# Two hybrid decoder layers on Trainium2: mixer steps cut to 128 columns and traced in another order

## The chip, the cores and the metric

The kernel runs on one core of a Trainium2 chip. The metric is the device time of one execution in microseconds. Engines: PE (TensorE, matmuls), DVE (VectorE), ACT (ScalarE), POOL (GpSimd), and SP, whose queue issues the DMA transfers.

## What is computed

Two layers of a decoder trunk act on x of 256 tokens by 1024 features, modulated by a conditioning vector c. In short:

```python
for l in range(2):
    sh_m, sc_m, g_m, sh_f, sc_f, g_f = split(silu(c) @ ada_w[l] + ada_b[l])
    h = rms_norm(x, norm_mix[l]) * (1 + sc_m) + sh_m
    rw_cols, ssd_cols, fox_cols, gate_logits = split(h @ w_in[l])
    y_rw  = rwkv7(rw_cols)    # token shift, decay, delta-rule state over 256 steps, 8 heads of 64
    y_ssd = ssd(ssd_cols)     # conv of 4 taps, chunked state-space scan, 16 heads in 4 groups
    y_fox = fox(fox_cols)     # causal softmax attention with forget gates, 8 heads
    merged = sum(sigmoid(gate_b) * (y_b @ proj_b))
    x = x + g_m * (merged @ w_out[l])
    h = rms_norm(x, norm_ffn[l]) * (1 + sc_f) + sh_f
    x = x + g_f * FFN(h)      # layer 0: SwiGLU; layer 1: the best 2 of 8 SwiGLU experts
```

All products are in float32 precision: both operands are split into a high and a low part, and three matmuls of the parts are summed.

## The kernel before, in words

Time runs through six stages: start, mixer of layer 0 (about 60 to 485 us of the span), its output projection and the dense FFN, mixer of layer 1 (about 720 to 1165 us), its output projection, and the experts.

A **mixer** consists of steps that share the engines. Every weight block comes by a DMA from SP's queue into one of three `raw` tiles. `accumulate` (L369) has ACT copy it to the high part (L157) and DVE subtract to the low part (L158), each 128x512 at a time, into five pairs of tiles; then PE multiplies 24 times for 128 columns (8 blocks of 128 features, three products each, 256 tokens wide). `stationary` (L379) does that for two blocks of 128 columns and calls what evacuates each from PSUM. PSUM has two `pd` banks for projections, four `pm` and two `ps`.

The steps and their names in the order string:
- `rw` and `r0`, `r1`: `rwkv_half` (L489) does four heads. Stages: projections of k, r and v with token shift (L451, L452), then the decay and key work up to masked matrices (L515 to L620; the mask copies are L615 on DVE), then the **levels** (L627 to L699), state and output (L700 to L752), gating (L753 to the end). The levels invert a triangular matrix in six doublings. In each, POOL masks (L632), PE multiplies, DVE transposes 32x32 blocks out of PSUM (L658), PE multiplies, DVE adds (L665), PE transposes, ACT copies (L675). The next doubling needs the result.
- `sd` and `s0` to `s3`: `ssd_group` (L798) with three stages: four blocks of projection with convolution (L808, L811, L813, L814), the chunk products (L831 to L867), the gate columns (L873 to L875) and the norm.
- `fx` and `f0`, `f1`: `fox_half` (L913): q, k and v by `project_rows` (L393), then attention of two pairs of heads.
- `G`: `gates` (L980), the first branch's gate columns, evacuated at L978. `m0`, `m1`, `m2`: `merge` (L989), the three branches' gate and output columns, evacuated at L1008 or L1010 and L1011.
- `mo` and `md`: `mod_next` (L293) loads 512 columns of a later modulation weight (L211) and sums them on DVE (L224, L226). `gm` puts a modulation row together.

Each of these functions is a generator, and `stages` (L438) makes the next call go on to the next `yield`. The loop at L1389 walks through `ORDER[l]` (L51) and runs one stage for each word. The string thus sets the order in which instructions are traced. The program is built with `schedule_with_timeline_sim=True`: a list scheduler then fixes the order of instructions on each engine, in which an instruction traced earlier goes first among those that are ready. On the chip each engine follows its fixed order and waits on semaphores.

Of the kernel before, what the change touches and what calls it, by code (L numbers as in the profile page):

```python
# [18 lines left out]
P = 128  # L19
# [44 lines left out]
def trunk(  # L64
# [314 lines left out]
    def stationary(raw, n, evac):  # L379

        ps = dbank()
        for q in range(0, n, P):
            m = min(P, n - q)
            o = ps[:m, q * 2:q * 2 + T]
            accumulate(o, raw[:, :, q:q + m], (hh, hl))
            evac(q // P, o)

    def project_cols(wsrc, c0, n, evac):
        for p0 in range(0, n, 256):
            w = min(256, n - p0)  # L390
            stationary(load_raw(rows(wsrc, 0, D, c0 + p0, w), KD, w), w, lambda i, ps: evac(p0 // P + i, ps))

    def project_rows(wsrc, c0, y):  # L393
# [3 lines left out]
        for kg in range(4):  # L397
            hi, lo = split_part(raw[:, 2 * kg:2 * kg + 2, :])
            for t in range(2):
                tb = slice(t * P, (t + 1) * P)  # L400
                for k in range(2):
                    kt = 2 * kg + k
                    mm3(ps[t], (y[0][:, kt, tb], y[1][:, kt, tb]), (hi[:, k, :], lo[:, k, :]), kt == 0, kt == KD - 1)
        return ps
# [67 lines left out]
    def rwkv(mx, l, prm, lora, gl):  # L472
        wa = mx("wa", [P, T])
        project_cols(w_in[l], 1536, 256, lambda i, ps: shift(prm, wa if i == 0 else gl[:, 0, :], ps, 12 + i))
# [12 lines left out]
        return [y[:, 0], y[:, 1]], lambda jp: stages(rwkv_half)(mx, l, prm, lora, jp, wa, gl, vup, y)  # L487

    def rwkv_half(mx, l, prm, lora, jp, wa, gl, vup, y):  # L489
# [8 lines left out]
        for dst, g in ((k, 1), (r, 0), (v, 2)):  # L498
            project_cols(w_in[l], g * RW + jp * 256, 256, lambda i, ps: shift(prm, dst[:, i, :], ps, 4 * g + 2 * jp + i))
# [11 lines left out]
        yield  # L511

        s, th = u(), u()
        for jj in J:
            js = slice((2 * jp + jj) * P, (2 * jp + jj + 1) * P)  # L515
            for dst, hb, base in ((s, 0, W0), (th, 1, A0)):
                ps = mbank()[:, :T]
                mm(ps, wau[hblock(hb), js], wa[hblock(hb), :])
                act.activation(dst[:, jj, :], ps, AF.Tanh, scale=0.5, bias=col(pph, base, jj))
        dve.tensor_scalar_add(s, s, 1.0)  # L520
# [10 lines left out]
        dve.tensor_tensor(L8, L8, mid.unsqueeze(2).broadcast_to([P, 4, P]), op=ALU.subtract)  # L531
        e1, e3, e2 = u(), u(), u()
# [4 lines left out]


# [6 lines left out]
        for t in range(2):  # L545
            for jj in J:
                mm(ps[:, t * 4 + 2 * jj:t * 4 + 2 * jj + 2], sq[:, jj, t * P:(t + 1) * P], headsel)
        ss, rs = small(8, "r"), small(8, "r")
# [9 lines left out]


# [10 lines left out]
        for jj in J:  # L570
            cv = "p (c t) -> p c t"
            dve.scalar_tensor_tensor(ar[jj][:, :, 0, :], kk[:, jj, :].rearrange(cv, c=2), -1.0, e2[:, jj, :].rearrange(cv, c=2), op0=ALU.mult, op1=ALU.mult)
            dve.tensor_mul(ar[jj][:, :, 1, :], r[:, jj, :].rearrange(cv, c=2), e1[:, jj, :].rearrange(cv, c=2))
        rk = u()
# [8 lines left out]


# [11 lines left out]

        s0 = mx("s0", [P, 2, 64])
# [5 lines left out]
        for ch in range(2):  # L603
# [4 lines left out]
            for dst, src in ((mats[:, 0], bt), (mats[:, 1], kt)):  # L608
# [29 lines left out]
        for ch in range(2):  # L638
# [4 lines left out]
            tms.append(tm)  # L643
        for ch in range(2):
            pz = level(ch, 0, icomp)
            tts[ch] = sq128()
            dve.tensor_add(tts[ch], pz, icomp)
        for ch in range(2):
# [3 lines left out]
            act.activation(tls[ch], pz, AF.Copy)  # L652
        for lv in range(1, 6):
            odd = slice(1, 4, 2) if lv == 5 else slice(0, 4)
            for ch in range(2):
                pz = level(ch, lv, tls[ch])
                for q in range(4):
                    dve.transpose(blk(bds[ch], q)[:, odd, bcol(q)], by4(blk(pz, q))[:, odd, :])  # L658
            for ch in range(2):
# [7 lines left out]
                else:  # L667
                    for n in (1, 3):
                        act.activation(blk(tms[ch], n)[:, :, bcol(n - 1)], by4(blk(pz, n)), AF.Copy)
            for ch in range(2):  # L670
# [5 lines left out]
                if lv == 4:  # L676
                    for n in range(4):
                        pool.tensor_copy(blk(tms[ch], n)[:, :, bcol(n)], by4(blk(tls[ch], n)))
        for ch in range(2):
# [4 lines left out]
            act.activation(ums[ch], pz, AF.Copy)  # L684
        h0, h1 = slice(0, 64), slice(64, 128)
        yas = []
        for ch in range(2):
# [4 lines left out]
            act.activation(yas[ch][h1], py[h1], AF.Copy)  # L692
        for ch in range(2):
# [5 lines left out]
        yield  # L699
        for ch in range(2):  # L700
# [23 lines left out]
            act.activation(sa, psa[:, 0:4, :], AF.Copy)  # L724
            if ch == 0:
# [12 lines left out]


# [10 lines left out]
            dve.tensor_scalar(var, var, 1.0 / 64, GN_EPS, op0=ALU.mult, op1=ALU.add)  # L750
            rsq(rs, var)
            dve.tensor_tensor(yg, yg, bc(rs), op=ALU.mult)  # L752
        yield  # L753
        pg = mbank()
        for jj in J:
            js = slice((2 * jp + jj) * P, (2 * jp + jj + 1) * P)
            mm(pg[:, jj * T:(jj + 1) * T], gu0[:, js], gl[:, 0, :], True, False)
            mm(pg[:, jj * T:(jj + 1) * T], gu1[:, js], gl[:, 1, :], False, True)
        yt = u()
# [11 lines left out]
    def ssd(mx, l, prm, dtr):  # L771
# [24 lines left out]
        return [yh, yl], lambda g: stages(ssd_group)(mx, l, prm, g, dt, cum, ac, dte, yh, yl)  # L796

    def ssd_group(mx, l, prm, g, dt, cum, ac, dte, yh, yl):  # L798
# [20 lines left out]
        stationary(raw, 256, lambda i, ps: conv(2 + i, ps))  # L819
        project_cols(w_in[l], XBC_OFF + g * 256, 256, conv)  # L820

        yield
# [7 lines left out]
        for ch in range(2):  # L830
            dve.tensor_tensor(xdt[:, ch, :].rearrange(h64, f=64), ps[:, ch, :].rearrange(h64, f=64),  # L831
                              hc(dt, ch).unsqueeze(2).broadcast_to([P, 4, 64]), op=ALU.mult)

# [5 lines left out]
        act.activation(cb[:, 2, :], ps[:, 1, :], AF.Copy)  # L839

        wms = [sv(4, P) for _ in range(3)]
        for b in range(2):
# [5 lines left out]
            for e in range(2):  # L848
# [3 lines left out]
                act.activation(wms[2][:, h, :], pc[:, e, 1, :], AF.Exp, bias=dte[:, 4 * g + h:4 * g + h + 1])  # L852
        for i in range(3):
            if i < 2:
                act.activation(wms[i], wms[i], AF.Exp, scale=-1.0)
            dve.tensor_tensor(wms[i], wms[i], cb[:, i, :].unsqueeze(1).broadcast_to([P, 4, P]), op=ALU.mult)
        y1 = sv(2, T)
# [11 lines left out]
        yield  # L869
# [7 lines left out]
        project_cols(w_in[l], SSD_OFF + g * 256, 256, gate)  # L877
# [8 lines left out]
        dve.tensor_scalar(ss, ps[:, 0:2], 1.0 / 256, EPS, op0=ALU.mult, op1=ALU.add)  # L886
        rsq(rs, ss)
# [9 lines left out]
    def fox(mx, l, prm, dtr):  # L897
# [13 lines left out]
        return [y[:, 0], y[:, 1]], lambda hf: stages(fox_half)(mx, l, qg, sums, hf, y)  # L911

    def fox_half(mx, l, qg, sums, hf, y):  # L913
# [3 lines left out]
        for g in range(3):  # L917
            ps = project_rows(w_in[l], FOX_OFF + 16 + g * 512 + hf * 256, (hh, hl))
# [11 lines left out]
            qkv.append(o)  # L930
        dve.tensor_scalar(ss, ss, 1.0 / 64, EPS, op0=ALU.mult, op1=ALU.add)
# [4 lines left out]
        for jj in range(2):  # L936
            yield
            j = 2 * hf + jj
            ka, qa = unit(mx, 2, T), unit(mx, 2, T)
            for e in range(2):  # L940
# [6 lines left out]
                act.activation(qa[0:65, e, :], ps[0:65, T:], AF.Copy, scale=qg[0:65, 0:1])  # L947
            po = mbank()[:, :T]
            for t in range(2):
                n = P * (t + 1)  # L950
                psc = mbank().rearrange("p (e k) -> p e k", e=2)
                for e in range(2):
                    mm(psc[:, e, :n], qa[0:65, e, t * P:(t + 1) * P], ka[0:65, e, :n], True, False)
                    mm(psc[:, e, t * P:n], identb, nmq, False, True)
                nmx, sm, rc = small(2, "f", 9), small(2, "f", 9), small(2, "f", 9)
# [5 lines left out]
                dve.tensor_tensor(pr[:, :, :n], pr[:, :, :n], rc.unsqueeze(2).broadcast_to([P, 2, n]), op=ALU.mult)  # L961
                pt = mbank().rearrange("p (e s q) -> p e s q", e=2, s=2)
# [550 lines left out]
```

## Time and profile before

| | us |
|---|---|
| median of 3 runs (lowest, highest) | 2197.69 (2197.65, 2198.89) |
| the profiled execution's own time | 2193.99 |
| its span, first to last instruction | 2192.2 |
| PE, DVE, ACT, POOL busy | 2075.0, 1799.2, 1380.4, 155.5 |
| instructions | 35360 |

The busy times overlap, so they add up to more than the span. A matmul counts as busy from its start to the modelled end of its result, so PE can be counted busy although it could take more. PEclk is the clock that TensorE was granted, as a share of its full speed. Line numbers are those of the kernel before.

### The profile page before, as it was taken

Reading aid. Unit: us, or ns where it says so; the run is one execution under the profiler, and the core shown is the slowest. Engines: PE = TensorE matmul, PEld = TensorE weight load, DVE = VectorE, ACT = ScalarE, POOL = GpSimd, SP = SyncE. Lnnn points to the kernel's source line nnn. Section 1 sums busy time; section 2 is a strip of 40 time slices with the busy share of each in tenths; the row PEclk is TensorE's granted clock in tenths of the full one; section 3 lists DMA queues with packets and bytes.
Section 4 is the critical chain, followed back from the end, with each engine's and each line's share of the span. In section 5 each row is a group of like instructions: output and inputs, shape, how many; then the busy total and the mean of one; then the engine's idle time right before and its main releaser. Section 6 shows DMA issues by size and latency. Waiting matters only on the chain.

```text
span 2192.2 us, 35360 instructions
## 1 busy us (share of the span) xinstructions
PE 2075.0 (95%) x13301; PEld 1797.9 (82%) x13301; DVE 1799.2 (82%) x2822; ACT 1380.4 (63%) x2204; POOL 155.5 (7%) x187
## 2 busy tenths in 40 slices
PE   6888899999997979989998999999999999999998
PEld 4778799999996868869998788888888887888776
DVE  4877777778776797857768999999999989998887
ACT  3445465555454536536556787777788777777775
POOL 2211210000000031210002000000000000000000
PEclk8999999999998889999998999999999999999999
DMA  8433355667884333415567999999999999999994
GB/s 292 126 94 90 96 177 191 204 211 256 285 290 157 113 100 107 145 49 169 190 198 261 349 372 355 329 348 385 368 332 365 354 350 352 338 352 367 343 352 168
DMA packets 313874, 546.77 MB, mean 249 GB/s; under 512 B 9856, under 2 KB 141056, under 8 KB 313696
## 3 DMA queue, kind: packets, MB, share of 16 engines
q1 hardware_dynamic: 313696, 544.44, 71.8%
q8 instruction: 106, 1.74, 0.3%
q14 instruction: 72, 0.59, 0.1%
HBM read 543.36 MB, written 1.05 MB: 248 GB/s over the span
## 4 chain that ended last, share of the span: by engine, by line
PE 80%; DVE 12%; issue 3%; DMA 3%; ACT 2%; POOL 0%; SPq 0%; DVEq 0%; ACTq 0%; POOLq 0%
PE pd L123 38%; PE pm L123 32%; PE ps L123 7%; DVE lo L158 5%; DVE u L658 2%; PE pm L132 2%; DMA araw<-in_ada_w_dram 1%; PE ps L132 1%; ACT hi L157 1%; DVE cu L811 1%; DMA b<-in_ada_w_dram 1%; DMA raw<-in_moe_w_gu_dram 0%; DVE b L615 0%; DVE xr L1270 0%; DMA raw<-in_proj_ssd_dram 0%
## 5 line engine op out<-in xcount | busy, mean ns | idle before, releaser
L157 ACT ACTIVATE hi<-raw 128x1024 fp32r<-128x1024 f32 (+2 forms) x1200 | 1024.6, 871 | 496.0 <-PE pd L123 257.0
L158 DVE TENSOR_TENSOR lo<-raw,hi 128x1024 fp32r<-128x1024 f32 (+2 forms) x1196 | 1153.9, 992 | 194.4 <-ACT hi L157 176.2
L123 PE MATMUL pd<-hh,hi 128*128 128x256 f32 (+1 forms) x1184 | 350.2, 296 | 20.8 <-DVE cu L811 5.2
L123 PE MATMUL pd<-hl,hi 128*128 128x256 f32 (+1 forms) x1184 | 342.2, 289 | 0.8 <-DVE hl L365 0.8
L123 PE MATMUL pd<-hh,lo 128*128 128x256 f32 (+1 forms) x1184 | 341.2, 289 | 0.0
L123 PE MATMUL pm<-lo,hh 128*128 128x512 f32 x672 | 266.7, 397 | 2.7 <-DVE lo L158 2.5
L123 PE MATMUL pm<-hi,hh 128*128 128x512 f32 x672 | 265.9, 396 | 0.3 <-ACT hi L157 0.2
L123 PE MATMUL pm<-hi,hl 128*128 128x512 f32 x672 | 262.4, 391 | 0.0
L123 PEld LDWEIGHTS pd<-hh,hi 128*128 128x128 f32 (+1 forms) x1184 | 231.9, 196 | 34.8 <-issue 7.2
L123 PEld LDWEIGHTS pd<-hl,hi 128*128 128x128 f32 (+1 forms) x1184 | 232.7, 196 | 5.7 <-DVE hl L365 2.7
L123 PEld LDWEIGHTS pd<-hh,lo 128*128 128x128 f32 (+1 forms) x1184 | 232.2, 196 | 2.1 <-issue 1.3
L123 PE MATMUL pd<-lo,hi 128*128 128x512 f32 x448 | 175.0, 391 | 0.0
L123 PE MATMUL pd<-hi,hi 128*128 128x512 f32 x448 | 169.9, 391 | 0.0
L123 PE MATMUL pd<-hi,lo 128*128 128x512 f32 x448 | 168.2, 390 | 0.0
L123 PEld LDWEIGHTS pm<-lo,hh 128*128 128x128 f32 x672 | 126.3, 188 | 32.3 <-DVE lo L158 5.8
L123 PEld LDWEIGHTS pm<-hi,hh 128*128 128x128 f32 x672 | 126.2, 188 | 29.3 <-ACT hi L157 1.4
L123 PEld LDWEIGHTS pm<-hi,hl 128*128 128x128 f32 x672 | 126.3, 188 | 26.1
L123 PE MATMUL pm<-hi,more 128*128 128x512 f32 x448 | 142.0, 392 | 0.0
L123 PEld LDWEIGHTS pd<-hi,hi 128*128 128x128 f32 x448 | 84.1, 188 | 18.2 <-ACT hi L407 0.3
L123 PEld LDWEIGHTS pd<-hi,lo 128*128 128x128 f32 x448 | 84.0, 188 | 17.8 <-DVE lo L408 0.2
L123 PEld LDWEIGHTS pm<-hi,more 128*128 128x128 f32 x448 | 84.1, 188 | 17.5 <-ACT hi L157 0.3
L123 PEld LDWEIGHTS pd<-lo,hi 128*128 128x128 f32 x448 | 84.1, 188 | 17.5
(429 smaller groups left out, 3428.7 us busy)
## 6 DMA issues: line engine op xcount, KB each, us to landing
raw<-in_moe_w_gu_dram SPq DMA_DIRECT2D x224, 1024.0 KB, 6.9
raw<-in_moe_w_down_dram SPq DMA_DIRECT2D x110, 1024.0 KB, 6.9
raw<-in_w_in_dram SPq DMA_DIRECT2D x66, 1024.0 KB, 5.4
araw<-in_ada_w_dram SPq DMA_DIRECT2D x68, 512.0 KB, 4.7
raw<-in_ffn_w_gu_dram SPq DMA_DIRECT2D x22, 1024.0 KB, 7.3
raw<-in_ffn_w_down_dram SPq DMA_DIRECT2D x11, 1024.0 KB, 6.6
raw<-in_w_in_dram SPq DMA_DIRECT2D x16, 512.0 KB, 5.2
raw<-in_proj_ssd_dram SPq DMA_DIRECT2D x8, 1024.0 KB, 5.4
```

What stands on the lines that cost most here:

```text
L123: pe.matmul(o, lhsT, rhs, start=start, stop=stop)
L132: pe.transpose(o, i, ident[:n, :n])
L157: act.activation(hi, raw, AF.Copy)
L158: minus.tensor_sub(lo, raw, hi.bitcast(F32))
L658: dve.transpose(blk(bds[ch], q)[:, odd, bcol(q)], by4(blk(pz, q))[:, odd, :])
L811: dve.scalar_tensor_tensor(cu[:, s:T], ps[:, 0:T - s], pph[:, w:w + 1], cu[:, s:T], op0=ALU.mult, op1=ALU.add)
```

## The change

The mixers' functions yield more often: after each 128-column block of a projection, and between the parts of the RWKV, SSD, FoX and gate work. One RWKV half has 56 steps in place of 5, one SSD group 14 in place of 3, one run of gates or merges 8 in place of 4. `stages` is gone, and `small_cols` becomes a word of the string (`sc`). The instructions are the same. `ORDER` becomes two strings in which `r0*47` means 47 steps in a row.

```diff
-ORDER = [
-    (
-        "rw r0 r0 mo r0 r0 fx sd s0 s0 s0 s1 s1 s1 r1 r1 r1 r0 s2 mo s2 s2 f0 r1 r1 s3 mo G f0 mo G s3 s3 G "
-        "f0 G m0 f1 m0 f1 m0 md md m1 md m0 m1 m1 md f1 md md md m1 m2 gm m2 md m2 m2"
-    ).split(),
-    (
-        "rw r0 r0 mo r0 sd s0 s0 r0 r0 s0 s1 mo s1 s1 s2 r1 r1 G r1 s2 fx r1 G s2 r1 G s3 s3 mo f0 f0 s3 G m0 "
-        "f0 m0 mo m0 m0 f1 md f1 m1 m1 md md md gm m1 md m1 f1 m2 m2 m2 md md md m2"
-    ).split(),
-]
+ORDER = (
+    "sc rw r0*7 mo r0*47 fx sd s0*13 s1*5 r1*6 s1*3 r1*14 s1*5 s0 s1 r1*7 r0 r1*9 r0 s2*2 f0 s2*2 r1*5 s2*3 f0*3 r1 f0*2 r1*7 s2*3 mo s2*2 r1*2 s2 r1*2 s3*2 f0 s3 r1*2 mo G*2 f0*2 s3*2 f0*4 mo G*2 s3 r1 s3*5 s2 s3*3 G*2 f0*9 G f1 G f1 m0*3 f1 m0 f1*6 m0*2 f1 md f1*3 m1*3 md m1 md m0*2 m1*3 md f1*8 md m1*5 md m1*2 md f1 m1*2 m2*4 gm m2*4 md m2*8",
+    "sc rw r0*21 mo r0*8 sd r0*3 s0 r0 s0*3 r0 s0 r0 s0 r0*2 s0*3 r0 s0 r0*18 s0*4 s1*5 mo s1*7 s2 s1 s2*4 r1*6 s1 r1*13 G*2 r1*4 s2 fx r1*7 G s2 r1*2 s2*2 r1*17 s2*5 r1*2 G r1*4 s3 G*2 r1 s3*8 f0 mo f0*3 s3 f0*10 s3*4 G*2 m0*2 f0*8 m0*2 mo m0*2 f1 m0*2 f1*5 md f1*5 m1*4 f1*3 m1*4 md*3 gm m1*4 md m1*4 f1*8 m2*12 md*3 m2*4",
+)
...
             accumulate(o, raw[:, :, q:q + m], (hh, hl))
             evac(q // P, o)
+            yield
...
-    def stages(f):
-
-        def start(*a):
-            g = f(*a)
-            return lambda: next(g, None)
-        return start
+    def whole(g):
+
+        while True:
+            try:
+                next(g)
+            except StopIteration as e:
+                return e.value
...
         for dst, g in ((k, 1), (r, 0), (v, 2)):
-            project_cols(w_in[l], g * RW + jp * 256, 256, lambda i, ps: shift(prm, dst[:, i, :], ps, 4 * g + 2 * jp + i))
+            yield from project_cols(w_in[l], g * RW + jp * 256, 256, lambda i, ps, g=g, dst=dst: shift(prm, dst[:, i, :], ps, 4 * g + 2 * jp + i))
...
-            for step in ORDER[l]:
+            for word in ORDER[l].split():
+                name, _, n = word.partition("*")
+                for _ in range(int(n or 1)):
+                    take(name)
```

## Rows read from the trace of the kernel before

**Rows 1.** The page: busy time, share of the span and instructions of each engine.

```profile
PE 2075.0 (95%) x13301; PEld 1797.9 (82%) x13301; DVE 1799.2 (82%) x2822; ACT 1380.4 (63%) x2204; POOL 155.5 (7%) x187
```

**Rows 2.** Stretches: length; busy (count) PE, PEld, DVE, ACT, POOL; clock, DMA share, GB/s.

```profile
60.00:290.00 230.00, 204.08 (x1830) 178.59 (x1830) 181.01 (x403) 111.77 (x268) 52.59 (x59) 0.94 0.35 106
735.00:1000.00 265.00, 233.38 (x2027) 204.10 (x2026) 210.31 (x456) 131.96 (x312) 58.50 (x62) 0.92 0.36 106
...
60.00:108.00 48.00, 42.59 (x312) 37.35 (x312) 43.33 (x82) 22.02 (x46) 13.44 (x12) 0.93 0.41 122
...
205.00:260.00 55.00, 47.24 (x452) 37.17 (x450) 41.53 (x102) 21.52 (x56) 20.07 (x26) 0.94 0.20 58
295.00:485.00 190.00, 189.38 (x1623) 183.94 (x1623) 142.82 (x278) 113.22 (x249) 5.45 (x6) 1.00 0.61 197
...
775.00:830.00 55.00, 44.34 (x422) 37.14 (x420) 48.45 (x112) 23.64 (x58) 19.74 (x20) 0.84 0.34 103
920.00:990.00 70.00, 57.24 (x556) 45.80 (x556) 45.17 (x110) 28.09 (x73) 18.75 (x23) 0.92 0.20 60
990.00:1165.00 175.00, 171.49 (x1430) 166.18 (x1429) 127.60 (x232) 101.74 (x210) 17.96 (x13) 0.99 0.62 203
```

**Rows 3.** Waits of PE, first 775 to 830 us, then 920 to 990 us.

```profile
PE pm L123 <- DVE u L658: 5.3, 4, 3.2
PE pd L123 <- DVE zt L874: 4.1, 1, 4.1
...
PE pm L123 <- DVE u L658: 4.3, 7, 0.9
```

**Rows 4.** Groups of instructions on DVE, 775 to 830 us.

```profile
L158 DVE TENSOR_TENSOR lo<-raw,hi 128x512 fp32r<-128x512 f32 x15 | 13.0, 869 | 2.3 <-ACT hi L157 2.2
L658 DVE STREAM_TRANSPOSE u<-pm 32x128 f32<-32x128 f32 (+1 forms) x40 | 11.9, 298 | 1.2 <-PE pm L123 0.7
```

**Rows 5.** Timeline of DVE, 115 to 121 us: start, duration, instruction.

```profile
115.86 0.28 DVE L665 TENSOR_TENSOR c<-c,pm 128x128 f32<-128x128 f32 x1
...
116.83 0.41 DVE L874 SCALAR_TENSOR_TENSOR zt<-zt,pd 128x256 f32<-128x256 f32 x1
119.48 0.69 DVE L158 TENSOR_TENSOR lo<-raw,hi 128x512 fp32r<-128x512 f32 x1 [2.23 <-ACT hi L157]
120.55 0.65 DVE L658 STREAM_TRANSPOSE u<-pm 32x128 f32<-32x128 f32 x2 [0.38 <-PE pm L123]
```

**Rows 6.** Timeline of PE from 78 us, two matmuls of a projection.

```profile
78.66 0.28 PE L123 MATMUL pd<-hh,hi 128*128 128x256 f32 x1
78.78 0.28 PE L123 MATMUL pd<-hl,hi 128*128 128x256 f32 x1
```

**Rows 7.** Timelines of SP's DMA issues and of DVE, layer 0.

```profile
31.80 1.09 SPq L211 DMA_DIRECT2D araw<-in_ada_w_dram  x2
...
90.80 17.84 SPq L211 DMA_DIRECT2D araw<-in_ada_w_dram  x4
...
90.02 0.75 DVE L226 SCALAR_TENSOR_TENSOR u<-araw,silc,u 128x512 f32<-128x512 f32 x1
90.69 0.73 DVE L615 COPY_PREDICATED b<-mmask,pm 128x512 f32<-128x512 uint8 x1
```

**Rows 8.** Timeline of DVE: RWKV's last split, first merge, layer 1.

```profile
995.70 0.69 DVE L408 TENSOR_TENSOR b<-u,b 128x512 fp32r<-128x512 f32 x1
...
1010.01 0.42 DVE L1008 SCALAR_TENSOR_TENSOR b<-b,pd 128x256 f32<-128x256 f32 x1 [0.34 <-PE pd L123]
```

**Rows 9.** Timelines of DVE and POOL from 782 us; a POOL group, 60 to 485 us.

```profile
782.99 0.47 DVE L811 SCALAR_TENSOR_TENSOR cu<-pd,pph,cu 128x255 f32<-128x255 f32 x1
...
784.48 3.20 DVE L158 TENSOR_TENSOR lo<-raw,hi 128x512 fp32r<-128x512 f32 x2
...
782.85 4.28 POOL L632 TENSOR_TENSOR u<-b,ztm 128x512 f32<-128x512 f32 x3
...
L632 POOL TENSOR_TENSOR u<-b,ztm 128x512 f32<-128x512 f32 x24 | 30.1, 1274 | 50.9 <-PE pm L123 30.6 <-DVE b L615 20.3
```

More of the change, by code (lines that the diff above doesn't have):

```diff
@@ L390, in project_cols @@
             w = min(256, n - p0)
-            stationary(load_raw(rows(wsrc, 0, D, c0 + p0, w), KD, w), w, lambda i, ps: evac(p0 // P + i, ps))
+            yield from stationary(load_raw(rows(wsrc, 0, D, c0 + p0, w), KD, w), w, lambda i, ps, i0=p0 // P: evac(i0 + i, ps))
     def project_rows(wsrc, c0, y):
@@ L536, in rwkv_half @@
         act.activation(e2, s, AF.Exp, scale=-KAPPA)
+        yield
         kk = u()
@@ L557, in rwkv_half @@
         dve.tensor_mul(kk, kk, ps)
+        yield
         kn = u()
@@ L643, in rwkv_half @@
             tms.append(tm)
+        yield
         for ch in range(2):
@@ L647, in rwkv_half @@
             dve.tensor_add(tts[ch], pz, icomp)
+        yield
         for ch in range(2):
@@ L875, in gate @@
             dve.scalar_tensor_tensor(y1[:, i, :], y1[:, i, :], 0.5, zt, op0=ALU.mult, op1=ALU.mult)
-        project_cols(w_in[l], SSD_OFF + g * 256, 256, gate)
+        yield from project_cols(w_in[l], SSD_OFF + g * 256, 256, gate)
         sq = sv(2, T)
@@ L1385, in trunk, with part, take @@
                         prev = same
-            dtr, gl = small_cols(l, mx, prm)
-            run = {}
-            for step in ORDER[l]:
+            run, made = {}, {"y": [None] * 3}
+            done = object()
+            def part(step):
                 i = int(step[1]) if step[1:] in tuple("0123") else 0
-                if step == "rw":
-                    y_rw, rw = rwkv(mx, l, prm, lora, gl)
+                if step == "G":
+                    made["merged"] = mx("b8", [P, KD, T], bufs=NB8)
+                    return gates(mx, l, prm, 0, made["merged"])
+                if step[0] == "m":
+                    return merge(mx, l, prm, i, made["merged"], made["y"][i], (proj_rw, proj_ssd, proj_fox)[i][l], (4, 8, 4)[i], i == 0)
+                return made[step[0]](i)
+            def take(step):
+                if step == "sc":
+                    made["dt"], made["gl"] = small_cols(l, mx, prm)
+                elif step == "rw":
+                    made["y"][0], made["r"] = rwkv(mx, l, prm, lora, made["gl"])
                 elif step == "sd":
-                    y_ssd, sd = ssd(mx, l, prm, dtr)
+                    made["y"][1], made["s"] = ssd(mx, l, prm, made["dt"])
                 elif step == "fx":
-                    y_fox, fx = fox(mx, l, prm, dtr)
+                    made["y"][2], made["f"] = fox(mx, l, prm, made["dt"])
                 elif step == "mo":
@@ L1404, in trunk @@
                     gm = keep("vfirst", [P, 2, 512]) if l == 1 else mx("u2", [P, 2, 512])
[L1405 to L1406 removed]
+                    made["gm"] = [gm[:, 0], gm[:, 1]]
+                    mod_row(lambda: unit(mx, 4, P), l, 2, 0.5, made["gm"])
                 else:
                     if step not in run:
[L1409 to L1418 removed]
+                        run[step] = part(step)
+                    assert run[step] is not None, step
+                    if next(run[step], done) is done:
+                        run[step] = None
+                    return
+                assert step in ("mo", "md") or run.setdefault(step, None) is None, step
+            for word in ORDER[l].split():
+                name, _, n = word.partition("*")
+                for _ in range(int(n or 1)):
+                    take(name)
+            assert all(next(g, done) is done for g in run.values() if g)
+            merged, gm = made["merged"], made["gm"]
             dump(f"merged{l}", merged)
```

80 lines of the change are left out of this document (51 added, 29 removed).

## The prediction

> **What bounds the kernel now.** I read the busy shares first: PE is busy for 95% of the span and DVE for 82% [rows 1], so TensorE is the bound, and the question is where it is not at work. The busy time by stretches answers that [rows 2]. The order string reaches the two mixers alone, and the second half of each is full: PE works 189.38 of 190 us from 295 to 485, and 171.49 of 175 from 990 to 1165, at a granted clock of 1.00 and 0.99. What is open lies in the first half of each mixer. From 60 to 290 us PE is idle for 230 - 204.08 = 25.9 us, from 735 to 1000 for 265 - 233.38 = 31.6 us, and the granted clock there, a mean of its two levels 1.2 and 2.4 GHz, is 0.94 and 0.92 of the upper one. Weighing the busy time with what is missing (0.06 x 204 + 0.08 x 233) gives 31 us more. So no order of the same instructions can win more than about 88 us of 2194. Half of the idle time lies in the three stretches in which an RWKV half works on its levels and I expect a difference: 7.8 us from 205 to 260, 10.7 from 775 to 830, 12.8 from 920 to 990.
>
> What holds PE there is the list of its waits [rows 3]. From 775 to 830 and from 920 to 990 the first name is the DVE transpose of the triangular levels (L658), with 5.3 us and 4.3 us, then other DVE results. The levels are a chain PE, DVE, PE, ACT. One RWKV half puts 40 such transposes on DVE, 11.9 us [rows 4], and while they hold DVE, DVE does not split weights for the projections with which PE could be filled. From 205 to 260 DVE is busy 41.53 us of 55 and from 775 to 830 48.45 of 55: in the levels DVE, not PE, is short.
>
> **How the order acts.** No instruction, byte or matmul is added or taken away. Only the order of tracing changes, and that is a preference. The trace of before shows that an engine does not follow it strictly: in layer 0 SSD group 0 is traced behind the whole of RWKV's first half, yet its gate evacuation (L874, at 116.83 us) runs between two steps of that half's levels (L665 at 115.86, L658 at 120.55) [rows 5]. An earlier place in the string is a first claim on an engine, a later place means that a step fills gaps. A yield alone changes nothing.
>
> **The change part by part.** A step is now one 128-column block: 24 matmuls at 0.12 us start to start [rows 6], some 2.8 us of PE, for two splits of 0.69 us on DVE [rows 5] and two on ACT. An RWKV half has 56 steps: 7 of projections, 13 up to the masked matrices, 21 of levels, 13 of state and output, 2 of gating.
>
> (a) Layer 0, first half of RWKV. `r0*7 mo r0*47` is the old order but for `mo`, which moves from behind the second stage to behind the first. Two of its four transfers were issued at 31.80 us; the other two stand in SP's queue from 90.80 on, with two of the next `mo`, for the tiles that L226 frees, and hold the queue for 17.84 us [rows 7]. Asked for earlier, they may hold weight loads back in the same way; three raw tiles on hand cover that, and no row shows PE waiting for a weight transfer here, so I cost them at nothing. Its DVE work, eight L224 and L226, 8 x 0.75 us = 6.0 us at most, now has a claim before the chain up to the matrices, in a stretch where DVE is busy 43.33 of 48 us [rows 2]. The chain can come up to 6 us later; but the same work leaves the time from 90 us on, where it lies between the mask copies L615 (90.02 and 90.69) that the levels wait for [rows 7]. Bounds: 2 us gained, if a third of it had held the copies up, 6 lost. I take +2, nearer to the gain because DVE is loaded at both places.
>
> (b) Layer 0, 160 to 295. Seven of the fourteen steps of SSD group 1 fall behind the first 20 steps of RWKV's second half, and two pairs of steps of SSD group 2 and the first FoX step come ahead of the last five level steps; its state steps are strung between FoX, SSD 2 and SSD 3. Of the 7.8 us of idle from 205 to 260 I take back 3: the chain's first 16 level steps keep their claim on DVE. Bounds: nothing, and 7.8 us plus 0.06 x 47.24 = 2.8 us of clock.
>
> (c) Layer 1, first half of RWKV, 775 to 830. From level three on (`r0*3 s0 r0 s0*3 r0 ...`) each level step shares its claim with blocks of SSD group 0, which before had none until the levels were over. The waits for L658 (5.3 us) are of the kind that a block of 2.8 us covers; the wait of 4.1 us for L874 is not (see the first rival). I take 5 us of the idle and 2 of the 7.1 us of clock: -7. Bounds: 0, and 10.7 + 7.1 = 17.8 us. The Trainium skill (TensorE: Matmul & The Clock Gate, Terms) puts the price of a throttled clock at the throttled time by the missing share, which is 2 x 0.16 x 55 x 0.5 = 8.8 us as an estimate from that page; by it the term would be -7.5.
>
> (d) Layer 1, second half of RWKV, 920 to 990. The levels are cut by single steps of gates and SSD 2. Only a gate block brings PE work, and of those one more than before comes in ahead of the levels' end. I take 5 of the 12.8 us of idle. Bounds: 0, and 12.8 + 4.6 = 17.4 us.
>
> (e) The later strings (FoX, merges, SSD 3) lie in stretches that are full [rows 2]: nothing. If RWKV's second half ends later, the first merge is late next: in layer 1 it has 14 us to spare (y split at 995.70, first merge evacuation at 1010.01) [rows 8], and up to there other blocks cover it. I cost that at nothing.
>
> Sum: +2 - 3 - 7 - 5 = -13 us. The profiled execution took 2193.99 us (span 2192.2, 1.8 us around it), 3.7 us below the median of 2197.69; 2194 - 13 = 2181, as a median 2185 us. About 0.2% (4.4 us) is what a measurement of this kernel can tell from no change.
>
> **Rivals.** *Slower: splits under the masks.* While POOL multiplies the level masks (L632), a DVE instruction that reads two SBUF tiles takes twice as long: two splits take 3.20 us from 784.48 on, 1.60 each against 0.69 at 119.48 [rows 5], under three masks from 782.85 on, while L811 at 782.99, which reads PSUM and one tile, stays at 0.47 [rows 9]. PE's wait of 4.1 us for L874 ended just behind these. The 24 masks of layer 0's mixer take 30.1 us of POOL [rows 9], and layer 1 has as many. The change draws blocks, thus splits, into the levels; each one that lands under a mask costs 0.91 us on the engine that is short there. With 14 more of them the 13 us are gone; with 24, one for every second mask, it costs 22 us against a gain of 13, +9 us: 2207. It decides from about 20 on. Against it: the masks run as soon as their matrix is ready, three and more in a row, so many are done before the blocks come in. The Trainium skill (GPSIMD Engine Reference, Specifications) says that GpSimd contends with VectorE instructions of two SBUF inputs; by that rule only splits and products pay, not the transposes, and the rows agree (0.47 and 1.60). Chance 0.24.
>
> *No change.* If the readiness of data already decides the order, as rows 5 suggest, the new preferences shift work among gaps that stay as many: within 4 us of 2197. For it: the old string has nearly the same large order. Chance 0.14.
>
> *Large gain.* If three quarters of the gaps in the three level stretches close (idle 7.8 + 10.7 + 12.8, clock 2.8 + 7.1 + 4.6, 45.8 us in all), some 35 us go: 2163. Against it: DVE at 48.45 of 55 us leaves no room for the splits. Chance 0.12.
>
> **The numbers.** My forecast, 2185 us, has 0.50; its own range is 2172 to 2193. Faster by over 0.2%: 0.50 + 0.12 = 0.62; within it 0.14; slower 0.24. The range runs from 2162 (the large gain's middle) to 2208 (the slower rival's price): it leaves out half of the large gain and a third of the slower cases, about 0.14.
>
> **What would show it.** Right: the same counts per engine; PE's idle from 205 to 260, 775 to 830 and 920 to 990 smaller by 3 to 5 us each with a higher granted clock, the waits for L658 shorter, FFN and MoE as long as before. (a) is right if L226 runs before L615 and PE waits a little more before 90 us. The slower rival shows as a mean of L158 clearly over its 869 ns in the levels [rows 4] and PE waiting for splits or L874. The forecast is wrong if the mixers keep their length while gaps move to FoX or the merges, or if the first merge waits for RWKV.

## The result, and the profile after

The changed kernel takes 2174.7 us as the median of four runs (2171.73 to 2178.04), against 2197.67 for the kernel before beside it: ratio 0.9899, 95% interval [0.9877, 0.9921], so 23 us or 1.0% faster by the medians. A repeat (e9, below) gave 0.9895 [0.988, 0.991]. The forecast was 2185 us within 2162 to 2208: right in sign and range, but 13 us where 23 came between the medians.

The profiled execution took 2178.04 us with a span of 2176.1. Before's had taken 2193.99. This pair of traces differs by 16 us, and only that can be explained from them; the other 7 are that before's profiled run lies 3.7 us below its median and this one 3.3 above. First the page's busy times:

```profile
PE 2075.2 (95%) x13301; PEld 1798.0 (83%) x13301; DVE 1793.4 (82%) x2822; ACT 1379.5 (63%) x2204; POOL 158.0 (7%) x187
```

The counts are those of [rows 1] on every engine, and PE's busy time is the same within 0.2 us: nothing was added, and the time came from gaps and clock. The stretches, columns as in [rows 2], the ones of layer 1 taken 10 us earlier because that layer is ahead by then:

```profile
60.00:290.00 230.00, 209.31 (x1894) 182.57 (x1893) 185.40 (x420) 116.93 (x279) 54.85 (x61) 0.95 0.37 111
725.00:990.00 265.00, 238.95 (x2108) 211.97 (x2107) 214.25 (x469) 138.27 (x328) 59.27 (x62) 0.94 0.37 111
60.00:108.00 48.00, 42.87 (x316) 37.12 (x315) 41.68 (x83) 22.89 (x46) 10.21 (x11) 0.93 0.52 154
205.00:260.00 55.00, 46.76 (x456) 39.15 (x455) 41.32 (x96) 26.32 (x65) 17.06 (x20) 0.94 0.29 84
295.00:475.00 180.00, 179.41 (x1533) 173.98 (x1534) 136.03 (x264) 107.82 (x234) 3.89 (x5) 1.00 0.61 194
765.00:820.00 55.00, 47.26 (x452) 39.59 (x450) 47.27 (x113) 26.40 (x68) 18.66 (x20) 0.88 0.32 97
910.00:980.00 70.00, 60.45 (x597) 52.08 (x596) 51.18 (x122) 32.24 (x81) 20.58 (x22) 0.93 0.26 78
980.00:1150.00 170.00, 166.62 (x1390) 161.07 (x1389) 123.41 (x221) 98.90 (x206) 17.11 (x12) 0.99 0.64 210
```

PE's idle time from 60 to 290 us fell from 25.9 to 20.7 us, over layer 1's first 265 us from 31.6 to 26.1. In the levels of layer 1 the clock rose from 0.84 to 0.88, idle from 10.7 to 7.7 us; in those of the second half, idle from 12.8 to 9.6. From 205 to 260 nothing moved (47.24 to 46.76 busy). The full stretches are as full as they were. The waits of PE, first 765 to 820 us, then 910 to 980:

```profile
PE pd L117 <- DVE zt L900: 2.3, 1, 2.3
...
PE pm L117 <- DVE u L668: 1.3, 2, 1.0
...
PE pm L117 <- DVE u L668: 4.6, 6, 1.0
```

In the first stretch the waits for the transpose (L658 before, L668 now) went from 5.3 to 1.3 us and the one for the gate evacuation (L874, now L900) from 4.1 to 2.3 [rows 3]; in the second stretch the transposes' waits stayed, 4.3 and 4.6 us.

To see where time is won or lost I compare progress: for a moment T in before's trace, how much earlier has another kernel done as much matmul work (each matmul counted by its shape's start-to-start time, 0.05 to 0.227 us)? That is its lead, in us. It is worked out from the matmul records of the traces. As a measure of one trace it is good to about 1 us, and to 2 us among the small matmuls of the levels. Two executions of one order can differ by more, up to 5 us over layer 0's mixer (last section); and each trace is one execution, from 4 us under (e6) to 8 us over (e5, e11) its kernel's median. So a gain is read below from how the lead grows in a stretch, in all traces that have the order in question:

```
T before (us)    60    80   120   300   480   740   840   900  1000  1160  1180  2100
changed         1.4  -0.6   6.4   9.5   9.7   9.1  11.2  11.6  18.0  18.8  15.4  15.6
changed, again  0.2  -1.7   5.2   8.3   8.4  10.4  11.7  13.6  20.2  21.6  18.4  18.1
```

Four places: the lead grows by 7 us between 80 and 120 us, by 3 up to 300, by 2 to 3 from 740 to 900, by 6 to 7 from 900 to 1000. Then some 3 us are lost from 1160 to 1180, in the routing of the experts. The 7 us from 80 to 120 are where I had costed a loss.

### The profile page after: what moved, and what is told of

It is laid out like the page before. It is cut to its first block, busy times and chain, and to the rows that moved or that the text cites. A ratio compares the mean times of both kernels' runs of the same rounds, so it can differ in the third digit from the quotient of the medians.

```text
span 2176.1 us, 35338 instructions
## 1 busy us (share of the span) xinstructions
PE 2075.2 (95%) x13301; PEld 1798.0 (83%) x13301; DVE 1793.4 (82%) x2822; ACT 1379.5 (63%) x2204; POOL 158.0 (7%) x187
## 4 chain that ended last, share of the span: by engine, by line
PE 79%; DVE 12%; DMA 3%; issue 3%; ACT 2%; POOL 0%; SPq 0%; DVEq 0%; ACTq 0%; POOLq 0%
PE pd L117 37%; PE pm L117 32%; PE ps L117 7%; DVE lo L152 5%; DMA araw<-in_ada_w_dram 2%; DVE u L668 1%; PE pm L126 1%; PE ps L126 1%; ACT hi L151 1%; DVE cu L833 1%; DMA raw<-in_proj_ssd_dram 1%; DMA raw<-in_moe_w_gu_dram 0%; DVE xr L1304 0%; DVE macc L220 0%; DMA raw<-in_ada_w_dram 0%
```

## Experiments

**Batch 1: parts alone.** The theory to test was that each layer's gain is its own and comes from the parts I had costed; the rivals were that the parts don't add, and that the moved `mo`, which term (a) took as a small loss, is in truth a gain. All four kernels have the new, finer steps, with the old strings written in them. Finer steps alone do nothing in layer 0: e4, whose layer 0 has the old string, runs it in before's order on PE, DVE, ACT and POOL. Both old strings in finer steps were not run. Before took 2195.51 us here (median of 17).

`e1_mo_only`: the old strings, with layer 0's first `mo` moved.

```diff
-rw r0*20 mo r0*34 fx sd s0*14 s1*14 r1*41 ...
+rw r0*7 mo r0*47 fx sd s0*14 s1*14 r1*41 ...
```

> The old order, written in the new steps, with one edit: in layer 0 the modulation step (mo) goes from behind RWKV's second stage to behind its first. As predicted (term a): 0 to 6 us slower than before, I took 2. As the trace of after suggests (the same PE work is reached 0.6 us later at 80 us and 6.4 us earlier at 120 us): 4 to 5 us faster than before, and the eight sums L218 and L220 lie before 85 us. If the lead at 120 us is due to SSD group 1 and RWKV's second half, which also fill those gaps, this kernel is within 2 us of before.

Measured: 2193.27 us, ratio 0.9989 [0.9978, 1.0001]: by the medians not told from before, but the 2 us of loss that I had taken are outside the interval.

`e2_mo_back`: the changed kernel with only that `mo` put back.

```diff
-rw r0*7 mo r0*47 fx sd s0*13 s1*5 r1*6 ...
+rw r0*20 mo r0*34 fx sd s0*13 s1*5 r1*6 ...
```

> After, with the modulation step of layer 0 put back behind RWKV's second stage. By the prediction's term (a) 2 us faster than after; by the trace's reading 4 to 5 us slower than after, some 17 us faster than before; if the parts do not add up, neither of the two.

Measured: 2182.92 us, ratio 0.9946 [0.9933, 0.9959]. Without the move the change loses almost half its gain.

`e3_l0_new`: layer 0's new string with layer 1's old one. `e4_l1_new`: the reverse.

```diff
 ORDER = (
     "... the new string of layer 0",
-    "sc rw r0*21 mo r0*8 sd r0*3 s0 r0 s0*3 r0 s0 ...",
+    "sc rw r0*20 mo r0*21 sd s0*10 r0*15 s0*4 s1*5 ...",
```

> The new string in layer 0, the old order in layer 1. By the prediction 1 us faster than before; by the trace (layer 0's mixer ends 9.7 us earlier) 9 to 10 us faster. Layer 1's mixer keeps its length to within 1 us.

> The old order in layer 0, the new string in layer 1. By the prediction 12 us faster than before; by the trace 9 us in the mixer, of which 3 us may be lost where the experts' routing starts (there after's clock stays at its lower level for longer). Theory that the layers are independent: this gain and that of the kernel with the new string in layer 0 alone add up to after's gain within 3 us.

Measured: e3 2185.11 us, ratio 0.9953 [0.9939, 0.9966]; e4 2187.3 us, ratio 0.9962 [0.995, 0.9975]. The two gains, 10.4 and 8.2 us, make 18.6 of the 22 to 23: each layer does pay for itself. The leads of the four:

```
T before (us)    60    80   120   300   480   740   840   900  1000  1160  1180  2100
e1 mo only      1.6  -0.4   8.3   6.9   6.7   8.8   3.2   4.8   3.6   3.9   4.9   2.9
e2 mo back      1.8   1.6   1.9   3.8   4.2   5.4   6.7   8.9  15.3  16.2  12.9  12.3
e3 layer 0 new  1.9  -0.0   8.7  13.4  13.9  16.1  10.6  12.2  11.1  11.8   8.6   8.6
e4 layer 1 new  0.3   0.3  -0.3  -1.5  -1.5  -2.4   2.3  -3.0   3.5   4.7   2.6   0.9
```

Two readings. First, the moved `mo` is worth 6.7 us in layer 0's mixer by itself (e1) and 4 to 5.5 on top of the new string (the changed kernel's 8.4 and 9.7 less e2's 4.2). From 60 to 80 us every trace with the move loses 2 us, and from 80 to 120 it gains 7 to 9; e2 and e4, without it, change by less than 1. Second, e1 gives 5 us of it back between 740 and 1000 us, in layer 1, whose string it doesn't touch, and e3 loses 4 from 740 to 1160 (16.1 to 11.8), where I had expected layer 1 to keep its length. Their order there is not before's: the last three of the modulation sums, which before runs at 778.6, 783.4 and 788.3 us, run at 763.9, 766.8 and 769.7 in e1, between the mask copies. On PE and ACT e1 and e3 run layer 1 in one and the same order, another than before's. The likely reason is that the list scheduler works on the whole program and carries the moved step of layer 0 on into layer 1; whether the finer steps of layer 1 have a part in it was not tried. So "the parts don't add" holds too, at the size of some 5 us.

**Batch 2: the halves of layer 1, and two more moves.** Before took 2196.58 us here (median of 9).

`e5_l1_first` has layer 0 new and layer 1 new only to the end of SSD group 0; `e6_l1_second` has layer 1 old to there and new afterwards.

```diff
 e5: ... s0 r0 s0*3 r0 s0 r0 s0 r0*2 s0*3 r0 s0 r0*18 s0*4 s1*5 mo
-    s1*7 s2 s1 s2*4 r1*6 s1 r1*13 G*2 r1*4 s2 fx r1*7 G s2 ...
+    s1*9 s2*5 r1*20 G*2 r1*21 s2*5 fx r1*13 G*2 s2*4 ...
 e6:
-    sc rw r0*21 mo r0*8 sd r0*3 s0 r0 s0*3 r0 s0 r0 s0 r0*2 s0*3 r0 s0 r0*18 s0*4
+    sc rw r0*20 mo r0*21 sd s0*10 r0*15 s0*4
     s1*5 mo s1*7 s2 s1 s2*4 r1*6 s1 r1*13 G*2 r1*4 s2 fx r1*7 G s2 ...
```

> Layer 0 has the new string in full; layer 1 has the new string only up to the end of SSD group 0 (so RWKV's first half and its levels strung with SSD blocks), and from there the old one. Theory A (the blocks of SSD 0 drawn into the levels are what layer 1 gains, my term of 7 us): some 6 to 8 us under the kernel with layer 0 alone new (2185.1), so 2177 to 2179. Theory B (the two halves of layer 1's string do not add, because the compiler's list of ready work is reshuffled by each): anything from 2175 to 2187, and the lead at 840 us is not kept up to 1000 us.

> Layer 0 has the new string in full; layer 1 has the old string up to the end of SSD group 0 and from there the new one (RWKV's second half strung between SSD 2, gates and FoX). Theory A (my term of 5 us for 920 to 990): some 4 to 6 us under the kernel with layer 0 alone new (2185.1), so 2179 to 2181, with the lead growing between 900 and 1000 us. Theory B: no sum, 2180 to 2187, and the lead changes in places whose string is unchanged.

Measured: e5 2178.75 us, ratio 0.9915 [0.9899, 0.993]; e6 2176.41 us, ratio 0.9914 [0.9898, 0.9931]. By ratio each is some 8 us under e3's 0.9953; both together (the changed kernel, 0.9895 to 0.9899) some 12 to 13. With intervals of 3 us to either side these don't tell 12 from 17, so whether the halves add fully stays open. That each gives something is plain. The leads say where:

```
T before (us)    740   820   840   900  1000  1160
e3 neither      16.1  18.1  10.6  12.2  11.1  11.8
e5 first half    7.7  10.6   9.8  10.1   9.7  10.3
e6 second half  15.4  18.8  12.8  13.4  22.5  23.5
both (changed)   9.1  12.0  11.2  11.6  18.0  18.8
```

From 820 to 840 us every kernel with the old first half behind a layer 0 other than before's loses 6 to 8 us (e3, e6, e1 with 10.8 to 3.2, and e11 below with 10.7 to 4.6); those with the new one lose at most 1. From 900 to 1000 the new second half gains 6 to 9 us in all nine traces that have it, the old one loses 0.4 to 1.2. The same in the stretches, of e3 first:

```profile
765.00:820.00 55.00, 45.74 (x418) 38.28 (x416) 39.19 (x98) 24.66 (x66) 13.26 (x17) 0.81 0.28 85
820.00:840.00 20.00, 17.18 (x169) 15.81 (x169) 11.51 (x28) 11.02 (x29) 1.81 (x2) 0.91 0.18 54
...
910.00:980.00 70.00, 58.19 (x516) 48.55 (x515) 42.86 (x108) 27.78 (x74) 10.66 (x18) 0.83 0.20 60
```

then of e5:

```profile
765.00:820.00 55.00, 47.27 (x449) 39.50 (x450) 48.32 (x115) 25.18 (x63) 18.67 (x20) 0.88 0.33 97
820.00:840.00 20.00, 20.00 (x212) 18.72 (x213) 12.94 (x31) 13.25 (x37) 1.40 (x2) 1.00 0.18 56
```

and of e6:

```profile
910.00:980.00 70.00, 60.41 (x601) 52.25 (x600) 50.23 (x121) 35.18 (x88) 13.47 (x18) 0.98 0.30 91
```

With the SSD blocks strung into the levels DVE is busy 48.32 us of 55 instead of 39.19, and behind the levels PE is full (20.00 of 20 at clock 1.00) where e3 still has gaps. With the second half strung, PE's busy time rises by 2.2 us and the clock from 0.83 to 0.98. In these rows a level's gaps are thus paid for twice, in idle time and in clock.

`e7_mo_l1`: the changed kernel, layer 1's first `mo` moved as in layer 0.

```diff
-sc rw r0*21 mo r0*8 sd ...
+sc rw r0*7 mo r0*22 sd ...
```

> The changed kernel, with layer 1's first modulation step also moved from behind RWKV's matrix stage to behind its projections, as layer 0 has it. Theory C (in layer 0 most of the gain came from taking the modulation sums out of the stage in which VectorE is short): the same move in layer 1 takes its eight sums of 0.75 to 1.7 us away from 740 to 800 us, and gives 4 to 6 us: 2169 to 2171. Rival (layer 0 gains because its two transfers no longer hold the sync engine's queue before the levels, which in layer 1 does not occur): within 2 us of the changed kernel, 2173 to 2177.

Measured: 2176.47 us, ratio 0.9903 [0.9885, 0.9921]: no gain. The sums run from 726.90 us instead of 756.26, yet the lead falls from 7.8 at 740 us to 1.9 at 760 and is back at 9.2 by 840. From the first mask copy to the first level transpose it takes 13.6 us (766.03 to 779.61) where the changed kernel takes 21.0 (757.54 to 778.56): the matrix stage gains 7.4 us, but it starts 8.5 later. The move costs ahead of the stage what it gives back in it.

`e8_lev0`: the changed kernel with layer 0's SSD group 0 strung into the first half's levels, too.

```diff
-rw r0*7 mo r0*47 fx sd s0*13 s1*5 ...
+rw r0*7 mo r0*22 fx sd r0*3 s0 r0 s0*3 r0 s0 r0 s0 r0*2 s0*3 r0 s0 r0*16 s0*3 s1*5 ...
```

> The changed kernel, with layer 0's first RWKV half strung with SSD group 0 in its levels as layer 1 has it (in layer 0 the change leaves SSD 0 behind the whole half). Theory A (blocks with a claim among the levels fill what the chain leaves open): PE's idle from 108 to 160 us, 52 less 47.3 us, falls by 2 to 4 us: 2170 to 2173. Theory B (an engine takes SSD 0's blocks into these gaps anyway, whatever the string says): within 2 us, 2173 to 2177. Slower rival (the blocks' splits fall under the masks at 1.6 in place of 0.69 us): 2178 or more, with the splits' mean clearly over 0.87 us from 105 to 160 us.

Measured: 2174.99 us, ratio 0.9905 [0.9889, 0.992], the same as the changed kernel. PE's busy time from 108 to 160 us is 47.53 us against 47.32. The other string hardly changed the program: by the traces DVE and POOL keep the changed kernel's order throughout, and PE's differs at 197 of the 5195 matmuls ahead of layer 1. The scheduler had put the blocks into these gaps whatever the string says, so theory B holds here and theory A was not put to a test.

**Batch 3: what of the moved `mo` pays.** `e9_after_again` is the changed kernel once more; before took 2195.37 us (median of 9).

> The changed kernel itself once more, on the chip of the two below, so that they are compared with it there and not over two chips, and for a second profile of the same instruction order. Expected 2172 to 2178 us. If the lead over the kernel before at the end of layer 0's mixer comes out between 9 and 14 us, as it did in five traces with the same order there (8.3 to 13.9), the spread belongs to the granted clock and not to any string.

Measured: 2172.7 us, ratio 0.9895 [0.988, 0.991]; its lead is in the first table. With 8.4 us at 480 it falls just short of the 9 to 14 I had set. Every engine runs the order of the changed kernel.

`e10_sums_late` was to cut the moved step in two, with the transfers early and the sums back in the old place.

```diff
-rw r0*7 mo r0*47 fx
+rw r0*7 ml r0*13 ma r0*34 fx
+elif step == "ml":
+    mod_load(mx, False)
+elif step == "ma":
+    mod_add(mx, *mod_raw.pop(0))
```

> The changed kernel with the moved step of layer 0 cut in two: its transfers stay behind RWKV's first 7 blocks, its eight VectorE sums go back to where the old order has them, behind the 20th. Theory C (the sums, not the transfers, are what the move takes out of the matrix stage): it behaves as the kernel with the whole step put back, 2181 to 2184 us, with L218 and L220 again between 85 and 107 us and a granted clock well under 1 at 100 to 130 us. Rival (the early transfers keep the sync engine's queue free at 90 us, and that gives the gain): within 2 us of the changed kernel.

Measured: 2185.37 us, ratio 0.9955 [0.9941, 0.9968], 13 us over e9 beside it and no better than e2. Its lead is 0.5 at 80 us and -2.0 at 120. But the edit did not do what was meant: PE, DVE, ACT and POOL run in e2's order throughout, and SP issues its transfers in the same order. SP's DMA issues from 20 to 100 us, the first line in the changed kernel, the other two in e10:

```profile
64.22 7.06 SPq L205 DMA_DIRECT2D araw<-in_ada_w_dram  x3
...
32.45 1.99 SPq L205 DMA_DIRECT2D araw<-in_ada_w_dram  x2
...
91.46 3.65 SPq L205 DMA_DIRECT2D araw<-in_ada_w_dram  x2
```

There are two `araw` tiles. Two transfers go at 32 us in both kernels, and the other two wait until sums free the tiles, so in e10 they stand in the queue from 91.46 on, as in [rows 7]. e10 is therefore e2 once more, a second measurement of what putting the step back costs (10 us there by the ratios, 13 here), and it does not part the sums from the held queue. The traces do. In e10 no wait of PE, DVE or ACT from 85 to 125 us ends with a transfer, and the weights are ahead: the load issued behind the held queue, at 109.85 us, has landed at 116.14, and the load before that one (landed at 93.17) is first split at 124.64. So it is the place of the sums. The timeline of DVE in the changed kernel (start, duration, instruction; L218 and L220 are the sums, L621 the mask copies):

```profile
62.24 0.48 DVE L218 TENSOR_SCALAR u<-araw,silc 128x512 f32<-128x512 f32 x1
63.45 0.75 DVE L220 SCALAR_TENSOR_TENSOR u<-araw,silc,u 128x512 f32<-128x512 f32 x1
...
74.28 0.73 DVE L220 SCALAR_TENSOR_TENSOR u<-araw,silc,u 128x512 f32<-128x512 f32 x1
...
94.72 1.34 DVE L621 COPY_PREDICATED b<-mmask,pm 128x512 f32<-128x512 uint8 x2 [0.17 <-PE pm L117]
...
109.52 1.28 DVE L668 STREAM_TRANSPOSE u<-pm 32x128 f32<-32x128 f32 x4
```

and of e10:

```profile
90.17 0.48 DVE L218 TENSOR_SCALAR u<-araw,silc 128x512 f32<-128x512 f32 x1
...
91.67 0.73 DVE L621 COPY_PREDICATED b<-mmask,pm 128x512 f32<-128x512 uint8 x1 [0.24 <-PE pm L117]
92.31 0.73 DVE L220 SCALAR_TENSOR_TENSOR u<-araw,silc,u 128x512 f32<-128x512 f32 x1
...
101.53 0.73 DVE L621 COPY_PREDICATED b<-mmask,pm 128x512 f32<-128x512 uint8 x1
...
102.53 0.73 DVE L621 COPY_PREDICATED b<-mmask,pm 128x512 f32<-128x512 uint8 x1
...
103.35 1.69 DVE L220 SCALAR_TENSOR_TENSOR u<-araw,silc,u 128x512 f32<-128x512 f32 x1
...
107.57 1.65 DVE L220 SCALAR_TENSOR_TENSOR u<-araw,silc,u 128x512 f32<-128x512 f32 x1
...
111.49 0.62 DVE L668 STREAM_TRANSPOSE u<-pm 32x128 f32<-32x128 f32 x2 [0.86 <-PE pm L117]
```

In e10 the sums stand between the mask copies, as they did in [rows 7], and from the first mask copy to the first level transpose 19.8 us go by (91.67 to 111.49). In the changed kernel it is 14.8 (94.72 to 109.52). The stage starts 3 us later and still ends 2 us earlier, because DVE has less to carry in it: from 85 to 108 us DVE is busy 18.65 us of 23 in the changed kernel, 21.38 in e10 and 22.75 in the kernel before. These stretches, in that order:

```profile
85.00:108.00 23.00, 20.31 (x131) 15.69 (x130) 18.65 (x35) 6.15 (x13) 8.57 (x10) 0.85 0.32 92
85.00:108.00 23.00, 21.82 (x132) 17.75 (x131) 21.38 (x36) 6.26 (x12) 10.22 (x10) 0.80 0.39 115
85.00:108.00 23.00, 20.40 (x133) 16.47 (x131) 22.75 (x38) 6.65 (x13) 10.90 (x10) 0.85 0.37 115
```

The last two sums in e10 take 1.69 and 1.65 us in place of 0.75, under POOL's masks (100.74 to 108.67 us). The Trainium skill (GPSIMD Engine Reference, Specifications) says that GpSimd contends for SBUF with VectorE instructions of two SBUF inputs; the rows agree, L220 reads two (1.69 us) and the mask copies at 101.53 and 102.53, of one PSUM tile and a mask, stay at 0.73.

`e11_lev0_l1s` puts e8's layer 0 and e6's layer 1 together, the two pieces whose traces led most.

> Layer 0 new, with SSD group 0 also strung into its first RWKV half's levels; layer 1 old up to the end of SSD group 0 and new from there. The two pieces gave in single traces 2.9 and 0.6 us more lead than the changed kernel in layer 1. If they add: 2170 to 2173, a version better than both kernels. If, as with the halves of layer 1's string so far, parts do not add: 2173 to 2178, the same as the changed kernel.

Measured: 2173.43 us, ratio 0.9901 [0.9886, 0.9916], the same as the changed kernel. Its layer 1 runs in e6's order, and e8's string hardly changes layer 0, so this is nearly e6 again. No version ran that beats the changed kernel beyond the intervals.

## Why the prediction was right or wrong

**The sum and its size.** By the pair of traces the terms come to -16 us where I had -13; by the medians it is -23. Of the 10 us missing there, 7 are no term at all, but which executions were profiled (3.7 and 3.3 us, above). The sum was closer than its terms, though: one failed in sign, one was too large, and one loss was not foreseen. That the number came so near is in part luck.

**(a) The moved `mo`: predicted +2, measured -5 to -7 by 120 us. This step failed.** By the medians, putting the step back into the changed kernel costs 10 us (e2) and 13 (e10). I had both ends in view: the chain up to the matrices later, and DVE relieved from 90 us on. The first I bounded at 6 us, and it costs 2 (lead 1.4 at 60 us, -0.6 at 80; in the repeat 0.2 and -1.7). The second I bounded at 2 us, "if a third of it had held the copies up", and it gives 7 (80 to 120 us). That third was a guess where rows were at hand: the sums lay in a stretch, 85 to 108 us, where DVE was busy 22.75 us of 23, between the very copies the levels wait for, and the last two of them at 1.69 and 1.65 us in place of 0.75. Of their 7.5 us there (0.47, five of 0.73 to 0.75, 1.69, 1.65) most were on the path. "DVE is loaded at both places" was the wrong ground: DVE was busy 43.33 us of 48 [rows 2] over the whole stretch, but the slack was nearly all in its first part. The transfers, which I had costed at nothing, indeed cost nothing in these traces. e7 shows that a full stretch alone doesn't decide. In layer 1, too, the changed kernel's sums lie between the mask copies, from 756.26 to 770.5 us, with DVE busy 13.41 us of 14 (756 to 770), and moving them shortens the stage by 7.4 us; but there the first mask copy comes 8.5 us later, where in layer 0 it came 3 later. DVE had about as much room where the sums went (busy 10.36 us of 13 in the kernel before, 62 to 75, and 13.71 of 16 in the changed kernel, 727 to 743), so why they cost more in layer 1 stays open.

**(b) Layer 0, 160 to 295: predicted -3, right in size.** From 120 to 300 us the lead grows by 3.1 us in the changed kernel and in its repeat (6.4 to 9.5, 5.2 to 8.3), by 1.9 in e2, which has this part without (a), and by 4.7 in e3; with the old string it falls by 1.2 to 1.4 (e4, e1). The place was not as I said: from 205 to 260 us PE's busy time is as before (47.24 and 46.76 us), the lead falls up to 240 us (2.3 in the changed kernel) and comes back by 260 (8.2). Which of the strung steps does it wasn't tried. (Behind the first 20 steps of RWKV's second half stand six steps of SSD group 1, not the seven I counted.)

**(c) The levels of layer 1's first half: predicted -7; -2 to -3 against before, but 6 to 8 against what would have been.** The waits for the transpose fell from 5.3 to 1.3 us as said, the idle time from 10.7 to 7.7 us and the clock rose from 0.84 to 0.88, so the mechanism holds and the size was off: 3 us of idle where I took 5. What I missed is that the old string, behind a layer 0 with the moved `mo`, loses 6 to 8 us at 820 to 840 us (e1, e3, e6), and the new one doesn't. The term was right as the worth of the string there, and too large as a difference from the trace of before. Behind before's own layer 0 (e4) the new string gains 4.7 us from 740 to 840 us and loses 5.3 by 900, so there it is worth nothing.

**(d) Layer 1's second half: predicted -5, measured -6.4 to -6.6 (the lead from 900 to 1000 us).** Idle fell by 3.2 us, from 12.8 to 9.6, where I took 5; the other half of the lead I can't place in one wait. The waits for the transpose are unchanged (4.3 and 4.6 us), so the gaps that were filled are others than those I named.

**(e) The later strings: nothing, as said.** The first merge found its operand: RWKV's last split is at 974.84 us and the first merge evacuation at 991.62, in [rows 8] 995.70 and 1010.01.

```profile
974.84 0.69 DVE L405 TENSOR_TENSOR b<-u,b 128x512 fp32r<-128x512 f32 x1
...
991.62 0.42 DVE L1042 SCALAR_TENSOR_TENSOR b<-b,pd 128x256 f32<-128x256 f32 x1
```

**The loss at the routing, which I had left out.** "FFN and MoE as long as before" was wrong by 3.3 us in these two traces. PE does the same work there. In before the last evacuation of the output projection behind the mixer (L1020) runs at 1169.7 us and the clock is back at 1.00 from 1185 on, 15 us later; in between it is partly up:

```profile
1165.00:1170.00 5.00, 5.00 (x26) 5.00 (x25) 5.00 (x6) 2.38 (x6) 1.58 (x1) 0.50 1.05 387
1170.00:1175.00 5.00, 5.00 (x30) 5.00 (x30) 4.80 (x12) 3.80 (x14) 0.00 (x0) 0.60 1.01 378
1175.00:1180.00 5.00, 2.63 (x27) 2.48 (x26) 2.41 (x14) 0.49 (x2) 0.71 (x1) 0.74 0.43 167
```

In the changed kernel that evacuation runs at 1150.8 us and the clock is back from 1171 on, 20 us later; it stays at its lower level, 1.2 GHz (0.50), through the same stretch:

```profile
1146.00:1151.00 5.00, 5.00 (x26) 5.00 (x26) 5.00 (x6) 2.38 (x6) 1.62 (x1) 0.50 1.05 389
1151.00:1156.00 5.00, 5.00 (x26) 5.00 (x25) 4.83 (x12) 3.80 (x14) 0.02 (x1) 0.50 1.02 392
1156.00:1161.00 5.00, 5.00 (x25) 5.00 (x24) 0.11 (x1) 0.00 (x0) 0.69 (x1) 0.50 0.43 164
```

With the clock down a stretch of 5 us holds 25 or 26 matmuls; before did 30 and 27 in its second and third, the third with PE idle for 2.37 us. Most of the traces lose 3 us or more from 1160 to 2100 us, e6 and e1 only about 1. The order of the instructions alone doesn't decide it: e1 and e3 run layer 1 in one order on PE, and e1 loses 1.0 us where e3 loses 3.2. What does stays open.

**The rivals.** *Splits under the masks* did not come. Durations of all splits on DVE (minimum, median, maximum in ns), in the changed kernel from 60 to 290 us and from 725 to 990:

```profile
L152 DVE TENSOR_TENSOR lo<-raw,hi x78: 660/684/1636, 60.9 to 289.0; 128x512 fp32r<-128x512 f32 x78
...
L152 DVE TENSOR_TENSOR lo<-raw,hi x93: 672/685/1659, 725.0 to 989.2; 128x512 fp32r<-128x512 f32 x93
```

Up to 1.66 us happens, but by the single records 9 and 8 splits lie under a mask in the two layers where it was 5 and 9 before: three more, not the twenty from which the rival decides. In the levels of layer 1 the splits' mean is 884 ns, where it was 869 [rows 4]. Its price of 1.6 us came up to it; the count was the guess. *No change* fell for the whole, though e8 shows it for one place. The *large gain* of 35 us didn't come: from 765 to 820 us DVE is still busy 47.27 us of 55, as long as PE (47.26).

## What to carry to other kernels

Before costing a move, look at how full the engine is in the few microseconds between which the moved work lies now, not over the whole stage: most of 7.5 us of sums on a DVE that was busy 22.75 of 23 us were on the path, and the same sums cost 2 us where DVE had slack. Look as hard at where the work goes: in layer 1 the same move gave 7.4 us and took 8.5. An order string is a preference for the whole program: a part measured alone can be given back in a layer it doesn't touch, so test a part both alone and by taking it out of the full change. Before reading an experiment, compare the order that its engines ran: e10 was e2 again, and e8 nearly the changed kernel. Compare medians of several runs with medians: one profiled execution of each kernel was off by 3 to 4 us on either side of a change of 23.

## What was not expected of the hardware

The same order of instructions runs layer 0's mixer in two ways. Six traces here have the changed kernel's layer 0, with the same order of instructions up to layer 1 on PE, DVE, ACT, POOL and SP: the changed kernel, its repeat, e5 and e7, with leads of 9.7, 8.4, 8.3 and 8.3 us at 480, and e3 and e6, with 13.9 and 13.4. They part at 90 us. e2 and e10, which share another order, do it too: 4.2 and -0.8 us at 480, parted by 120. Stretches of the changed kernel:

```profile
85.00:90.00 5.00, 2.72 (x22) 2.47 (x21) 5.00 (x12) 1.81 (x4) 1.66 (x4) 1.00 0.72 210
90.00:95.00 5.00, 4.60 (x20) 2.92 (x19) 4.83 (x11) 1.86 (x4) 0.34 (x1) 0.58 0.02 3
95.00:100.00 5.00, 5.00 (x27) 4.21 (x27) 3.20 (x6) 0.68 (x2) 1.24 (x1) 0.73 0.03 4
```

and of e3:

```profile
85.00:90.00 5.00, 2.71 (x21) 2.42 (x21) 5.00 (x12) 1.72 (x3) 1.99 (x4) 0.97 0.71 210
90.00:95.00 5.00, 5.00 (x27) 3.63 (x26) 5.00 (x11) 1.92 (x4) 0.00 (x0) 0.69 0.02 3
95.00:100.00 5.00, 5.00 (x29) 3.45 (x28) 4.14 (x7) 0.63 (x1) 1.24 (x1) 1.00 0.35 84
```

After the same light work from 85 to 90 us (PE busy 2.72 and 2.71 us) the clock falls to its lower level in both, but in e3 it is back at 1.00 from 95 us on, in the changed kernel only from 100. A lead of 2 us is gone by 120 us, and with later dips some 5 of a mixer of 430. What sets it apart stays open: e3 and e6 were profiled on two chips, and have in common the old first half of layer 1, which runs 600 us later; but e11 has that half too, and e3's order on every engine up to 127 us, and goes the slower way (8.0 us at 480). The Trainium skill (TensorE: Matmul & The Clock Gate, What's actually happening) says that the number of matmuls at the lower clock varies from run to run of one kernel; these traces don't contradict it: about 5 us lie between executions of one order in this mixer. The runs of the changed kernel spread by the like (2171.73 to 2178.04 us).
